# Seven block products for eight in the down projection of segments 1 to 3, and state updates on column halves

## The chip, the cores and the metric

The kernel runs on one core of one Trainium2 chip. The metric is the device time of one execution in microseconds: 3076.15 us, the median of three runs (3075.18 to 3080.12). A core has a matrix engine (PE; its weight loads are listed apart as PEld), a vector engine (DVE), a scalar engine (ACT), a general engine (POOL) and SP, which here issues all DMAs. Each engine takes its own queue in order; between engines there are semaphores.

## The reference

One layer of a streaming encoder on 2048 positions of width 1024, in float32, with 16 meta positions ahead. The part that is changed is the gated MLP at the end, and one matrix product inside the recurrence:

```python
z = rmsnorm(h, norm2_g[l])
u, v = jnp.split(z @ w_up[l], 2, axis=-1)        # D_FF = 2816 columns each: 22 blocks of 128
u = causal_dwconv(u, conv_w[l], conv_b[l])       # width 3, depthwise
h = h + (jax.nn.silu(u) * v) @ w_down[l]         # the down projection, 2816 x 1024
...
S = jnp.exp(a_last[:, :, 0, :])[..., None] * S + jnp.einsum('bhsk,bhsv->bhkv', k_ * jnp.exp(a_last - a_), v_)
```

After the MLP comes a last rmsnorm, and the meta positions are dropped.

## The kernel before

**Tiling.** The 2048 positions go through the whole layer in four segments of 512 (`s` = 0 to 3), each in four row chunks of 128. Every operand of a matrix product is split into a high and a low part (ACT casts the high part, L95 or L108; DVE subtracts for the low one, L96 or L109), and each block takes three matmuls (`PASS`: high x high, high x low, low x high). Weights come by DMA as `raw` tiles (3 buffers) and are split into `w` tiles (3 buffers).

**The MLP** goes through its 22 blocks `j` in groups (`GROUPS`: 8, 8 and 6). In segment 0 a block takes 24 matmuls of 512 columns for `u` and as many for the gate. At the same time `weight_sums` writes sums of weight blocks to DRAM (`s_d`, `a_d`); segments 1 to 3 use them: there `q_open` and `q_rest` build each block by seven products of half size (`seventh`, L779), the Strassen-Winograd scheme, 7 x 12 matmuls of 256 columns. Then DVE and ACT do the convolution, the sigmoid and the gate, and `gated` splits the result into an `act` tile (L109).

**The down projection** of a group follows its blocks in all segments: for each half `dh` of the output columns `rows_product` (L142) multiplies all `act` tiles of the group with the weights, 4 row chunks x 3 matmuls of 512 columns for each block, into four PSUM banks `rp`, which `add_d` then adds to the residual rows `h` (L898). For the very last half, `rows_one_by_one` (L130) goes chunk by chunk, so that `finish` (last rmsnorm and output) can start early.

**The turn of a segment.** Beside the down projection of the last group, the norm of the next segment's input runs: `norm1` hands out five steps (`between`), one at each weight load. A step loads a chunk of x into an `x_row` tile (`xt`, 2 buffers, L69), ACT sums its squares (L171), DVE takes twelve very small steps to the inverse root (`inv_rms`, tiles `nrm`) and scales the chunk (L214); the next step transposes it on PE (`norm1_transposes`, L217, PSUM tag `mm`) and splits it into the `z` tiles (32 per segment on ACT, L111, and 32 on DVE, L112). Then `values` (`rp<-w,z`, L274) starts the next segment and needs all of these.

**Order.** The code is written in the order of the computation; a list scheduler in the tile framework then sets the order of each engine's queue. PSUM has eight banks: tag `mm` has 5 and tag `hg` has 3. What a tile waits for is set by its pool: it gets a buffer when the last user of the buffer is done.

Of the kernel before, what the change touches and what calls it, by code (L numbers as in the profile page):

```python
# [26 lines left out]
GROUPS = ((0, 8), (8, 8), (16, 6))  # L27
# [22 lines left out]
def trunk_layer(ctx: ExitStack, tc: tile.TileContext, x, meta, wts, cst, gf, wpool, out):  # L50
# [79 lines left out]
    def rows_one_by_one(src, chunks, nk, consume):  # L130

        ws = [weights() for _ in range(nk // 2)]
        for ci, (o, n) in enumerate(chunks):
            bank = ps.tile([P, 512], F32, name="rp", tag="hg", bufs=HG)
            for k in range(nk):
                for i, (xi, wi) in enumerate(PASS):
                    T.matmul(bank[:n, :], lhsT=src[k][:, xi, o:o + n],
                             rhs=ws[k // 2][:, wi, (k % 2) * 512:(k % 2 + 1) * 512],
                             start=(k == 0 and i == 0), stop=(k == nk - 1 and i == 2))
            consume(ci, bank)  # L140

    def rows_product(src, chunks, nk, consume, between=(), lo=None, hg=HG):  # L142
# [362 lines left out]
    a_d = [dram.tile([2, P, 2, 512], F32, name=f"a_d{j}") for j in range(NF)]  # L505
    for s in range(nseg):
# [476 lines left out]
```

## Time and profile before

| | |
|---|---|
| median of 3 runs | 3076.15 us |
| the profiled execution, its own time | 3076.68 us |
| its span, first to last instruction | 3074.9 us |
| PE busy | 3023.7 us (98%), 21452 matmuls |
| DVE busy | 1977.5 us (64%) |
| ACT busy | 1296.2 us (42%) |
| DMA | 439.99 MB, 143 GB/s on the mean |

PE's matmuls are pipelined: one of 512 columns is listed with some 390 ns, but in a row they start about 231 ns apart. So the distance from start to start counts, not the length of one. The same holds on DVE, where the next instruction often starts before the listed end of the one before. An average over the run mixes stages; the windows in the rows below are single stages.

### The profile page before, as it was taken

How to read it: one execution, taken by the hardware profiler on the slowest of the kernel's cores; microseconds unless marked ns; L12 is line 12 of the kernel's file. 1: busy time of each engine (PE TensorE's matmuls, PEld its weight loads, DVE VectorE, ACT ScalarE, POOL GpSimd, SP SyncE). 2: the span in 40 equal slices, each digit the busy share in tenths (PEclk: the TensorE clock that was granted, in tenths of full speed). 3: DMA queues.
4: the chain of work that ended last, by engine and by line, in shares of the span. 5: the costliest groups of instructions: out<-in, count | busy, mean ns of one | idle time of the engine just before them, and what ended most of it. 6: DMA issues, size and time to landing. Idle time of an engine off the chain costs nothing.

```text
span 3074.9 us, 51974 instructions
## 1 busy us (share of the span) xinstructions
PE 3023.7 (98%) x21452; PEld 2627.1 (85%) x21452; DVE 1977.5 (64%) x3366; ACT 1296.2 (42%) x2130; POOL 69.3 (2%) x180
## 2 busy tenths in 40 slices
PE   7999999999999999999999999999999999999998
PEld 6999978898887788989987778899898778888987
DVE  5875357565768735857577753685576883485756
ACT  4443234232543424635454332554354432364534
POOL 1000000000000000000000000000000000000000
PEclk9999999999999999999999999999999999999999
DMA  3112238474532225646452222655454212364643
GB/s 142 63 63 76 90 122 292 170 265 175 194 132 70 76 96 165 224 156 218 136 181 74 69 84 96 225 200 171 164 166 151 70 64 95 123 214 167 225 149 110
DMA packets 146497, 439.99 MB, mean 143 GB/s; under 512 B 14018, under 2 KB 14146, under 8 KB 146260
## 3 DMA queue, kind: packets, MB, share of 16 engines
q1 hardware_dynamic: 146260, 436.67, 41.7%
q8 instruction: 168, 2.75, 0.4%
q14 instruction: 69, 0.57, 0.1%
HBM read 382.09 MB, written 54.53 MB: 142 GB/s over the span
## 4 chain that ended last, share of the span: by engine, by line
PE 93%; DVE 3%; DMA 1%; ACT 1%; issue 0%; SPq 0%; DVEq 0%; ACTq 0%
PE pt L124 36%; PE rp L153 22%; PE X L782 12%; PE Y L782 9%; PE pt L749 8%; DMA raw<-in_wts_dram 1%; PE sp L319 1%; PE up L394 1%; PE sp L331 1%; DVE w L96 1%; PE op L408 1%; PE op L413 1%; PE ktp L385 1%; DVE z L109 0%; PE pp L575 0%
## 5 line engine op out<-in xcount | busy, mean ns | idle before, releaser
L96 DVE TENSOR_TENSOR w<-raw,w 128x1024 fp32r<-128x1024 f32 (+1 forms) x607 | 706.6, 1165 | 727.8 <-ACT w L95 724.1
L124 PE MATMUL pt<-z,w 128*128 128x512 f32 (+3 forms) x4800 | 954.7, 354 | 0.0
L124 PEld LDWEIGHTS pt<-z,w 128*128 128x128 f32 x4800 | 773.4, 189 | 136.7 <-issue 12.8
L95 ACT CAST w<-raw 128x1024 fp32r<-128x1024 f32 (+1 forms) x611 | 610.8, 1000 | 650.9 <-PE rp L153 277.2
L153 PE MATMUL rp<-w,act 128*128 128x512 f32 x2040 | 477.2, 394 | 0.0
L153 PEld LDWEIGHTS rp<-w,act 128*128 128x128 f32 x2040 | 381.9, 188 | 87.1
L782 PE MATMUL X<-z,w 128*128 128x256 f32 x2484 | 339.3, 286 | 10.2 <-ACT z L108 5.5
L782 PEld LDWEIGHTS X<-z,w 128*128 128x128 f32 x2484 | 316.7, 194 | 14.3 <-ACT z L108 6.8
L749 PE MATMUL pt<-z,w 128*128 128x256 f32 (+2 forms) x1608 | 254.5, 320 | 0.0
L749 PEld LDWEIGHTS pt<-z,w 128*128 128x128 f32 x1608 | 229.9, 190 | 23.2
L782 PE MATMUL Y<-z,w 128*128 128x256 f32 x1692 | 233.7, 286 | 0.0
L782 PEld LDWEIGHTS Y<-z,w 128*128 128x128 f32 x1692 | 218.5, 195 | 0.3
L153 PE MATMUL rp<-w,mix 128*128 128x512 f32 (+1 forms) x816 | 190.4, 394 | 0.0
L153 PEld LDWEIGHTS rp<-w,mix 128*128 128x128 f32 (+1 forms) x816 | 147.9, 182 | 40.2 <-issue 4.7
L650 ACT ACTIVATE sg<-pt 128x512 f32<-128x512 f32 (+1 forms) x80 | 41.2, 515 | 243.1 <-PE pt L124 243.1
L734 DVE SCALAR_TENSOR_TENSOR cv<-ub,cs,cv 128x512 f32<-128x512 f32 x176 | 131.1, 745 | 0.7
L737 ACT ACTIVATE sg<-cv 128x512 f32<-128x512 f32 x88 | 55.7, 633 | 103.2 <-DVE cv L734 103.1
L153 PE MATMUL rp<-w,z 128*128 128x512 f32 (+1 forms) x408 | 97.9, 398 | 0.0
L124 PE MATMUL pt<-ob,w 128*128 128x512 f32 (+2 forms) x480 | 95.1, 350 | 0.0
L124 PE MATMUL pt<-oa,w 128*128 128x512 f32 (+2 forms) x480 | 94.8, 348 | 0.0
L153 PEld LDWEIGHTS rp<-w,z 128*128 128x128 f32 (+1 forms) x408 | 74.5, 183 | 19.6 <-issue 0.4
L782 PE MATMUL X<-z,wa 128*128 128x256 f32 x684 | 90.9, 281 | 0.0
(197 smaller groups left out, 2902.0 us busy)
## 6 DMA issues: line engine op xcount, KB each, us to landing
raw<-in_wts_dram SPq DMA_DIRECT2D x413, 512.0 KB, 3.5
raw<-s_d SPq DMA_DIRECT2D x132, 512.0 KB, 3.3
wa<-a_d SPq DMA_DIRECT2D x114, 512.0 KB, 5.2
s_d<-ws SPq DMA_DIRECT2D x44, 512.0 KB, 4.5
a_d<-w SPq DMA_DIRECT2D x44, 512.0 KB, 3.7
raw<-in_wts_dram SPq DMA_DIRECT2D x66, 256.0 KB, 3.1
h<-in_x_dram SPq DMA_DIRECT2D x20, 512.0 KB, 6.5
xt<-in_x_dram SPq DMA_DIRECT2D x12, 512.0 KB, 4.3
```

Source lines behind the costliest of these rows:

```text
L95: A.copy(out=w[:, 0, :n], in_=raw[:, :n])
L96: (lo or V).tensor_tensor(out=w[:, 1, :n], in0=raw[:, :n], in1=w[:, 0, :n].bitcast(F32), op=ALU.subtract)
L124: T.matmul(pt[:, :n], lhsT=w[:, wi, (kof + k) * P:(kof + k + 1) * P], rhs=src[k][:, xi, c0 + o:c0 + o + n], start=(k == 0 and i == 0), sto ...
L153: T.matmul(banks[ci][:n, :], lhsT=src[k][:, xi, o:o + n], rhs=w[:, wi, (k % 2) * 512:(k % 2 + 1) * 512], start=(k == 0 and i == 0), stop=( ...
L319: T.matmul(spv[o:o + B, e, c, :], lhsT=k[:, x], rhs=q[:, x], start=True, stop=True)
L331: T.matmul(spv[o:o + h_, e, c, :], lhsT=k[:, x:x + h_], rhs=q[:, x + h_:x + 2 * h_], start=True, stop=True)
L385: T.transpose(out=ktp[:C, c * P:(c + 1) * P], in_=kv[:, c * C:(c + 1) * C], identity=ident)
L650: A.activation(out=sg[:, o:o + n], in_=pt[:, :n], func=AF.Sigmoid)
L734: V.scalar_tensor_tensor(out=cv, in0=ub[:, t_:t_ + SEG], scalar=col(C_CW + t_ * NF, j), in1=cv, op0=ALU.mult, op1=ALU.add)
L737: A.activation(out=sg, in_=cv, func=AF.Sigmoid)
L749: T.matmul(pt[:, po:po + n], lhsT=w[:, wi, k * P:(k + 1) * P], rhs=z2[k][:, xi, c0:c0 + n], start=(k == 0 and i == 0), stop=(k == KB - 1 a ...
L782: T.matmul(dst, lhsT=w[:, wi, kp * P:(kp + 1) * P], rhs=z2[kp][:, xi, xslot], start=(start and kp == 0 and i == 0), stop=(kp == KP - 1 and ...
```

## The change

In segments 1 to 3 the down projection of a group takes seven products instead of eight, again by the Strassen-Winograd scheme. The 2 x 2 blocks are: rows in two halves (chunks 0, 1 and chunks 2, 3), and blocks `j` in pairs (even, odd) against the two halves of the output columns. For each pair of blocks `pair_operands` makes four sums of the gated results and splits what the products need (`act`, four tiles for a pair). The sums of down weights that the scheme needs are made in segment 0 by `down_sums` and written to DRAM (`t_d`). `down_sevenths` runs the seven products, each 3 `nj` matmuls of 512 columns, with its own weight load (`load`: two blocks of 512 columns in one tile), and adds its banks `dp` to `h` (16 adds of 128x512 for a group, 8 before). The groups become 6, 6, 4 and 6. `norm1_transposes` takes its banks from tag `hg`. Tag `am` gets 12 buffers (8 before), tag `zo` 4 (8 before), and `oa` moves to `am`. `pair_operands` keeps its sums in `x_row` tiles. The state update (`upv`) is issued as two matmuls of 64 weight columns for one of 128. `rows_one_by_one` goes.

```diff
@@ trunk_layer
-GROUPS = ((0, 8), (8, 8), (16, 6))
+GROUPS = ((0, 6), (6, 6), (12, 4), (16, 6))
...
-            tp = ps.tile([P, 512], F32, name="tp", tag="mm", bufs=MM)
+            tp = ps.tile([P, 512], F32, name="tp", tag="hg", bufs=HG)
...
-                T.matmul(upv[:, e, c, :], lhsT=kts[e][:C, c * P:(c + 1) * P], rhs=vt[c][:C, v0:v0 + VD],
-                         start=True, stop=True)
+                for d in range(0, P, VD):
+                    T.matmul(upv[d:d + VD, e, c, :], lhsT=kts[e][:C, c * P + d:c * P + d + VD],
+                             rhs=vt[c][:C, v0:v0 + VD], start=True, stop=True)
...
+    t_d = {j0: dram.tile([4, nj // 2, P, 512], F32, name=f"t_d{j0}") for (j0, nj) in GROUPS}
...
-            gated(cv, sy, a)
+            V.tensor_tensor(out=cv, in0=cv, in1=sy, op=ALU.mult)
+            return cv
...
+        def unit():
+            return blk.tile([P, 2, WMAX], F32R, name="act", tag="am", bufs=12)[:, :, :2 * HT].rearrange(
+                "p a (u t) -> p a u t", t=HT)
+
+        def pair_operands(c0, c1, u0):
+            a11, a21, a12, a22 = c0[:, :HT], c0[:, HT:], c1[:, :HT], c1[:, HT:]
+            t = x_row().rearrange("p (u t) -> p u t", t=HT)
+            u1, u2, u3 = unit(), unit(), unit()
+            V.tensor_tensor(out=t[:, 0], in0=a21, in1=a22, op=ALU.add)
+            V.tensor_tensor(out=t[:, 1], in0=a21, in1=a11, op=ALU.subtract)
+            V.tensor_tensor(out=t[:, 2], in0=t[:, 0], in1=a11, op=ALU.subtract)
+            V.tensor_tensor(out=t[:, 3], in0=a12, in1=t[:, 2], op=ALU.subtract)
+            split((u3[:, 0], u3[:, 1]), c1.rearrange("p (u t) -> p u t", t=HT))
+            split((u1[:, 0], u1[:, 1]), t[:, 0:2])
+            split((u2[:, 0], u2[:, 1]), t[:, 2:4])
+            return {"a11": u0[:, :, 0], "a12": u3[:, :, 0], "a22": u3[:, :, 1], "s1": u1[:, :, 0],
+                    "s3": u1[:, :, 1], "s2": u2[:, :, 0], "s4": u2[:, :, 1]}
+
+        def down_sums(j0, nj, dh):
+            def on_raw(i, raw):
+                if i % 2 != dh:
+                    return
+                other = wpl.tile([P, 1024], F32, name="raw", bufs=RAW)
+                nc.sync.dma_start(out=other, in_=wts[M_AT + 3 * j0 + 2 * nj + (1 - dh) * nj // 2 + i])
+                r0, r1 = (other, raw) if dh else (raw, other)
+                t = [blk.tile([P, 2 * WMAX], F32, name="ws", tag="zo", bufs=4)[:, :1024] for _ in range(2)]
+                V.tensor_tensor(out=t[0][:, :512], in0=r1[:, :512], in1=r0[:, :512], op=ALU.subtract)
+                V.tensor_tensor(out=t[0][:, 512:], in0=r1[:, :512], in1=r1[:, 512:], op=ALU.subtract)
+                V.tensor_tensor(out=t[1][:, :512], in0=r1[:, 512:], in1=t[0][:, :512], op=ALU.subtract)
+                V.tensor_tensor(out=t[1][:, 512:], in0=r0[:, 512:], in1=t[1][:, :512], op=ALU.subtract)
+                for o in range(4):
+                    nc.sync.dma_start(out=t_d[j0][o, i], in_=t[o // 2][:, o % 2 * 512:(o % 2 + 1) * 512])
+            return on_raw
+
+        def down_sevenths(ops, j0, nj, between, square, done):
+            nk, pc = nj // 2, M_AT + 3 * j0 + 2 * nj
...
+            def load(src):
+                ws = []
+                for i in range(0, nk, 2):
+                    n = min(2, nk - i)
+                    w = split_weights(src(i, i + n).rearrange("i p f -> p i f"), n * 512, view=True)[0]
+                    ws += [w[:, :, x * 512:(x + 1) * 512] for x in range(n)]
+                return ws
...
+            def product(banks, left, src, start, adds, order=0):
+                ws = load(src)
+                if between:
+                    between.pop(0)()
...
+                for kp, i in seq:
+                    for n, (xi, wi) in enumerate(PASS):
+                        T.matmul(banks[i], lhsT=ops[kp][left][:, xi, i * P:(i + 1) * P], rhs=ws[kp][:, wi, :],
+                                 start=(start and kp == 0 and n == 0), stop=(kp == nk - 1 and n == 2),
+                                 skip_group_check=True)
+                for i in range(2):
+                    for th, dh, final in adds:
+                        v = hx[2 * th + i][:, hcol[dh]]
+                        V.tensor_tensor(out=v, in0=v, in1=banks[i], op=ALU.add)
...
+            X = bank("mm")
+            product(X, "a11", nat(0, 0), True, ((0, 0, 0),))
+            product(bank("hg"), "a12", nat(0, 1), True, ((0, 0, 1),))
+            product(X, "s2", cat(2), False, ((0, 1, 0),))
+            Y = bank("mm")
+            product(Y, "s1", cat(0), True, ((1, 1, 0),))
+            product(X, "s3", cat(1), False, ((1, 1, 1), (1, 0, 0)))
+            product(Y, "s4", nat(1, 1), False, ((0, 1, 2),))
+            product(bank("hg"), "a22", cat(3), True, ((1, 0, 2),), order=1)
...
-                    q_rest(j, at_u(j) + 1, *opened.pop(j), act[j - j0])
+                    cv = q_rest(j, at_u(j) + 1, *opened.pop(j))
+                    if j % 2 == 0:
+                        even, u0 = cv, unit()
+                        split((u0[:, 0, 0], u0[:, 1, 0]), cv[:, :HT])
+                    else:
+                        ops.append(pair_operands(even, cv, u0))
...
-            for dh in range(2):
...
-                if end and dh == 1:
-                    rows_one_by_one(act, rows, nj, add_d)
-                else:
-                    rows_product(act, rows, nj, add_d, chunks)
+            if first_s:
+                for dh in range(2):
...
+                    rows_product(act, [(c * P, P) for c in range(NCH)], nj, add_d, chunks, on_raw=down_sums(j0, nj, dh))
+            else:
+                down_sevenths(ops, j0, nj, chunks, square, lambda ci: finish(ci, 1) if end else None)
```

Three places show how the queues change.

First, PE in the last group of segment 0 (`rp<-w,act` is its down projection, `tp` the transposes of the next input, `rp<-w,z` the start of the next segment). Before:

```order
L153 MATMUL rp<-w,act 128x512 x24
L221 MATMUL tp<-ident,xt 128x128 x8
L153 MATMUL rp<-w,act 128x512 x28
L221 MATMUL tp<-ident,xt 128x128 x8
L153 MATMUL rp<-w,act 128x512 x41
L221 MATMUL tp<-ident,xt 128x128 x8
L153 MATMUL rp<-w,act 128x512 x31
L221 MATMUL tp<-ident,xt 128x128 x8
L153 MATMUL rp<-w,act 128x512 x20
L153 MATMUL rp<-w,z 128x512 x96
```

and now:

```order
L144 MATMUL rp<-w,act 128x512 x67
L212 MATMUL tp<-ident,xt 128x128 x4
L144 MATMUL rp<-w,act 128x512
L212 MATMUL tp<-ident,xt 128x128 x4
L144 MATMUL rp<-w,act 128x512 x4
L212 MATMUL tp<-ident,xt 128x128 x16
L144 MATMUL rp<-w,act 128x512 x67
L212 MATMUL tp<-ident,xt 128x128 x4
L144 MATMUL rp<-w,act 128x512
L212 MATMUL tp<-ident,xt 128x128 x4
L144 MATMUL rp<-w,act 128x512 x4
L144 MATMUL rp<-w,z 128x512 x96
```

The transposes were spread over both halves of the down projection; now the first three chunks stand together between the two halves, and the last at the end.

Second, DVE at the end of the last group's blocks in segment 1 (`cv` is the gated result, `sy` the last read of a block's products, `act` splits, `nrm` the small steps of the norm, `xt` with `nrm` the scaling of a chunk of x, `w` the low part of a weight tile). Before, at the last block but one and the last:

```order
L109 TENSOR_TENSOR act_14270<-cv_14874,act_14270 128x512
L165 TENSOR_TENSOR nrm_15053<-nrm_15053 128x1
L166 SCALAR_TENSOR_TENSOR nrm_15053<-nrm_15053 128x1
...
L214 TENSOR_SCALAR xt_15046<-xt_15046,nrm_15053 128x1024
L96 TENSOR_TENSOR w_15039<-raw_15037,w_15039 128x1024
L814 TENSOR_TENSOR ub_14996<-Y_14907,sx_14908 128x512
L96 TENSOR_TENSOR w_15093<-raw_15091,w_15093 128x1024
L734 SCALAR_TENSOR_TENSOR cv_15000<-ub_14996,cs_91,cv_15000 128x512
L820 TENSOR_TENSOR sy_14981<-X_14906,sy_14981 128x512
```

and now, from the last block on:

```order
L814 TENSOR_TENSOR cv_15420<-cv_15420,sy_15401 128x512
L826 TENSOR_TENSOR xt_15446<-cv_15293,cv_15420 128x256
...
L109 TENSOR_TENSOR act_15448<-xt_15446,act_15448 128x512
L168 TENSOR_TENSOR nrm_15488<-ss_15483 128x1
...
L205 TENSOR_SCALAR xt_15481<-xt_15481,nrm_15488 128x1024
L168 TENSOR_TENSOR nrm_15567<-ss_15562 128x1
...
L155 SCALAR_TENSOR_TENSOR nrm_15567<-nrm_15567 128x1
L96 TENSOR_TENSOR w_15531<-raw_15529,w_15531 128x512
L883 TENSOR_TENSOR h1_11507<-h1_11507,dp_15465 128x512
L883 TENSOR_TENSOR h1_11509<-h1_11509,dp_15466 128x512
```

The norm of the first two chunks stood ahead of the last block's end; now it stands behind its splits, and ahead of the low part `w_15531` of the second product's last weight tile.

Third, DVE at the end of a group that is not the last, segment 1, from the last block's `sy` on. Before:

```order
L820 TENSOR_TENSOR sy<-X,sy 128x512
L734 SCALAR_TENSOR_TENSOR cv<-ub,cs,cv 128x512
L96 TENSOR_TENSOR w<-raw,w 128x1024
L738 TENSOR_TENSOR cv<-cv,sg 128x512
L742 TENSOR_TENSOR cv<-cv,sy 128x512
L109 TENSOR_TENSOR act<-cv,act 128x512
L96 TENSOR_TENSOR w<-raw,w 128x1024 x3
```

and now, in the group of four:

```order
L813 TENSOR_TENSOR sy<-X,sy 128x512
L727 SCALAR_TENSOR_TENSOR cv<-ub,cs,cv 128x512
L883 TENSOR_TENSOR h_11507<-h_11507,dp 128x512
L883 TENSOR_TENSOR h_11509<-h_11509,dp 128x512
L96 TENSOR_TENSOR w<-raw,w 128x1024
L731 TENSOR_TENSOR cv<-cv,sg 128x512
L96 TENSOR_TENSOR w<-raw,w 128x1024
L814 TENSOR_TENSOR cv<-cv,sy 128x512
L826 TENSOR_TENSOR xt<-cv 128x256
L828 TENSOR_TENSOR xt<-xt,cv 128x256
L109 TENSOR_TENSOR act<-cv,act 128x512
```

Between the last block's product and its split there are now two adds, two sums and one more weight tile.

## Rows read from the trace of the kernel before

**Rows 1.** The page, part 1, whole run: busy us (share) xinstructions.

```profile
span 3074.9 us, 51974 instructions
...
PE 3023.7 (98%) x21452; PEld 2627.1 (85%) x21452; DVE 1977.5 (64%) x3366; ACT 1296.2 (42%) x2130; POOL 69.3 (2%) x180
```

**Rows 2.** The page, part 4: the chain that ended last, by engine.

```profile
PE 93%; DVE 3%; DMA 1%; ACT 1%; issue 0%; SPq 0%; DVEq 0%; ACTq 0%
```

**Rows 3.** Groups by line, forms apart: count | busy us, mean ns | idle before.

```profile
L153 PE MATMUL rp<-w,act 128*128 128x512 f32 x2040 | 477.2, 394 | 0.0
```

**Rows 4.** Windows: from:to, length, PE PEld DVE ACT POOL busy, PEclk, DMA, GB/s.

```profile
1300.90:1321.04 20.14, 20.14 (x172) 20.14 (x170) 15.61 (x21) 12.05 (x21) 0.62 (x5) 1.00 0.75 249
1321.04:1365.45 44.41, 44.41 (x194) 36.09 (x193) 19.35 (x22) 10.00 (x11) 0.00 (x0) 1.00 0.33 111
1549.90:1587.20 37.30, 37.23 (x179) 30.44 (x178) 31.88 (x91) 25.04 (x63) 1.07 (x1) 1.00 0.47 156
810.10:847.00 36.90, 36.90 (x177) 30.20 (x176) 28.86 (x91) 23.77 (x61) 0.00 (x0) 1.00 0.40 129
...
3030.96:3064.50 33.54, 33.54 (x147) 26.98 (x145) 22.35 (x55) 10.75 (x21) 0.00 (x0) 1.00 0.26 91
```

**Rows 5.** Timeline, PE, last group of segment 1: start, length, instruction, count.

```profile
1555.46 1.03 PE L221 MATMUL tp<-ident,xt 128*128 128x128 f32 x8
...
1587.05 3.19 PE L153 MATMUL rp<-w,z 128*128 128x512 f32 x13
```

**Rows 6.** Timeline, DVE, segment 1: start us, length us, instruction, count.

```profile
1379.15 0.69 DVE L738 TENSOR_TENSOR cv<-cv,sg 128x512 f32<-128x512 f32 x1
1379.88 0.69 DVE L742 TENSOR_TENSOR cv<-cv,sy 128x512 f32<-128x512 f32 x1
...
1545.16 0.16 DVE L164 SCALAR_TENSOR_TENSOR nrm<-nrm 128x1 f32<-128x1 f32 x1
1545.36 0.16 DVE L165 TENSOR_TENSOR nrm<-nrm 128x1 f32<-128x1 f32 x1
...
1548.05 1.22 DVE L96 TENSOR_TENSOR w<-raw,w 128x1024 fp32r<-128x1024 f32 x1
1549.19 0.68 DVE L814 TENSOR_TENSOR ub<-Y,sx 128x512 f32<-128x512 f32 x1
...
1552.21 0.74 DVE L734 SCALAR_TENSOR_TENSOR cv<-ub,cs,cv 128x512 f32<-128x512 f32 x1
1552.87 1.22 DVE L96 TENSOR_TENSOR w<-raw,w 128x1024 fp32r<-128x1024 f32 x1
...
1558.19 0.60 DVE L112 SCALAR_TENSOR_TENSOR z<-tp,cs,z 128x128 fp32r<-128x128 f32 x2
...
1586.29 1.88 DVE L898 TENSOR_TENSOR h<-h,rp 128x512 f32<-128x512 f32 x3
```

**Rows 7.** Timeline, ACT, before the last group of segment 1.

```profile
1540.90 0.59 ACT L171 ACTIVATE jk<-xt 128x512 f32<-128x512 f32 x1
1541.44 0.19 ACT L171 ACTIVATION_READ_ACCUMULATOR jk<-xt 128x1 f32 x1
...
1545.10 0.62 ACT L108 CAST act<-cv 128x512 fp32r<-128x512 f32 x1 [0.37 <-DVE cv L742]
```

**Rows 8.** DMA issues, KB each, median us to landing.

```profile
xt<-in_x_dram SPq DMA_DIRECT2D x12, 512.0 KB, 4.3
```

**Rows 9.** Timeline, SP, early in the MLP of segment 1.

```profile
1240.01 0.38 SPq L209 DMA_DIRECT2D xt<-in_x_dram  x1
```

**Rows 10.** Windows, to_z2 in segment 1 (columns as in rows 4).

```profile
1246.35:1253.06 6.71, 3.41 (x16) 2.21 (x14) 4.89 (x8) 2.46 (x3) 0.00 (x0) 0.83 0.99 357
1253.06:1258.00 4.94, 4.94 (x25) 4.94 (x25) 1.23 (x1) 1.69 (x3) 0.00 (x0) 0.55 0.85 296
```

**Rows 11.** Timeline, PE, a state update in segment 1.

```profile
913.19 2.00 PE L394 MATMUL up<-vt,kt 128*128 128x64 f32 x16
...
917.06 0.39 PE L408 MATMUL op<-at,vt 128*64 128x128 f32 x4
```

More of the change, by code (lines that the diff above doesn't have):

```diff
@@ L128, in proj, with rows_product @@
         return res
[L130 to L142, printed above, removed]
+    def rows_product(src, chunks, nk, consume, between=(), lo=None, hg=HG, on_raw=None):
         banks = [ps.tile([P, 512], F32, name="rp", tag="hg", bufs=HG) if i < hg else
@@ L568, in trunk_layer @@
             chunks_out(p, q, k, tot, main, vt[-NCH:], False, o_raw)
-        ob = [blk.tile([P, 2, WMAX], F32R, name="ob", tag="zo") for _ in range(4)]
+        ob = [blk.tile([P, 2, WMAX], F32R, name="ob", tag="zo", bufs=4) for _ in range(4)]
         def group_product(g, dt):
@@ L620, in trunk_layer @@
         rsqrt(rs, ms, n1, n2)
-        rss = blk.tile([P, 2, WMAX], F32R, name="rss", tag="am")
+        rss = blk.tile([P, 2, WMAX], F32R, name="rss", tag="am", bufs=12)
         split((rss[:8, 0, :W1], rss[:8, 1, :W1]), rs)
-        oa = [blk.tile([P, 2, WMAX], F32R, name="oa", tag="zo") for _ in range(PAIRS)]
+        oa = [blk.tile([P, 2, WMAX], F32R, name="oa", tag="am", bufs=12) for _ in range(PAIRS)]
         for p in range(PAIRS):
@@ L640, in trunk_layer @@
             split((oa[p][:, 0, :W1], oa[p][:, 1, :W1]), t1[:, :W1])
-        mix = [blk.tile([P, 2, WMAX], F32R, name="mix", tag="am") for _ in range(KB)]
+        mix = [blk.tile([P, 2, WMAX], F32R, name="mix", tag="am", bufs=12) for _ in range(KB)]
         for d in range(KB):
@@ L790, in q_open @@
             else:
-                a11, a12 = (blk.tile([P, 2, WMAX], F32R, name="wa", tag="zo")[:, :, :512] for _ in range(2))
+                a11, a12 = (blk.tile([P, 2, WMAX], F32R, name="wa", tag="zo", bufs=4)[:, :, :512] for _ in range(2))
                 for i, a in enumerate((a11, a12)):
@@ L823, in trunk_layer @@
         for (j0, nj) in GROUPS:
-            act = [blk.tile([P, 2, WMAX], F32R, name="act", tag="am") for _ in range(nj)]
+            act = [blk.tile([P, 2, WMAX], F32R, name="act", tag="am", bufs=12) for _ in range(nj if first_s else 0)]
             at_u = lambda j: M_AT + 3 * j0 + 2 * (j - j0)
             if not first_s:
-                opened = {}
+                opened, ops = {}, []
                 for j in range(j0, j0 + nj):
@@ L893, in finish, with square, add_d @@
                         nc.sync.dma_start(out=out[s * SEG + c * P:s * SEG + (c + 1) * P], in_=hx[c])
-            for dh in range(2):
-                def add_d(ci, bank):
-                    v = hx[ci][:, dh * 512:(dh + 1) * 512]
-                    V.tensor_tensor(out=v, in0=v, in1=bank, op=ALU.add)
-                    if last:
-                        square_sums(ss[:, dh, ci:ci + 1], v, P)
-                    if end and dh == 1:
-                        finish(ci, 1)
-                rows = [(c * P, P) for c in range(NCH)]
-                if end and dh == 1:
-                    rows_one_by_one(act, rows, nj, add_d)
-                else:
-                    rows_product(act, rows, nj, add_d, chunks)
+            def square(ci, dh, v):
+                if last:
+                    square_sums(ss[:, dh, ci:ci + 1], v, P)
+            if first_s:
+                for dh in range(2):
+                    def add_d(ci, bank):
+                        v = hx[ci][:, dh * 512:(dh + 1) * 512]
+                        V.tensor_tensor(out=v, in0=v, in1=bank, op=ALU.add)
+                        square(ci, dh, v)
+                    rows_product(act, [(c * P, P) for c in range(NCH)], nj, add_d, chunks, on_raw=down_sums(j0, nj, dh))
+            else:
+                down_sevenths(ops, j0, nj, chunks, square, lambda ci: finish(ci, 1) if end else None)
             if last and not end:
```

34 lines of the change are left out of this document (24 added, 10 removed).

## The prediction

> **What bounds the kernel now.** I read the page's busy shares first, then the chain of waits, then single stages in windows. PE is busy for 98% of the span, and the chain that ended last is PE for 93% [rows 1, 2]; DVE has 64% on the mean. So the time is PE's, and the question for a change that takes matmuls off PE and gives work to DVE is whether DVE keeps up stage by stage. In the windows the reader is to look for PE's busy time against the length (no gap) and for DVE's beside it [rows 4]. The down projection of the first group of segment 1 takes 44.41 us for 192 matmuls, 0.231 us each, with DVE at 19.35. A stretch of two blocks has DVE at 15.61 of 20.14. But in the last group, where the norm of the next input runs beside it, DVE is at 31.88 of 37.30 (28.86 of 36.90 in segment 0) and PE has still no gap. That stage has nearly no room on DVE.
>
> **The change, part by part.** Time counts from T, when PE is done with a group's last block. DVE's steps are from start to start [rows 6]: a weight split of 1024 takes 1.14 us (1548.05 to 1549.19), an operation of 512 takes 0.60 (three adds in 1.88, the last 0.69 long) or 0.73 where it needs the one before, a convolution step 0.66, a small `nrm` step 0.20 in a chain, a `z` split 0.26 to 0.30. ACT casts 512 in 0.62 and squares half a chunk in 0.59 + 0.19 [rows 7]. For operations of 256 I take 0.4.
>
> *Matmuls.* Down projection: 24 matmuls for a block become 21; the lines that issue them are in [rows 3]. Saved are 3 x 22 x 3 segments = 198 x 0.231 = 45.8 us: 15.3 in a segment, 11.1 of it in the first three groups (16 blocks), 4.2 in the last.
>
> *First three groups.* For six blocks DVE now has 7 x (1.14 + 0.60) of weights and 16 x 0.60 of adds, 21.8 us, beside 126 x 0.231 = 29.1 of PE: room on the mean. But DVE works in order, and the second product's last third needs the last block's split. In the first group DVE's queue from T is `sy` 0.60, weights 0.60 and 1.14, convolution 0.66, weights 0.60, convolution 0.66, two adds 1.2, gate 0.73, weights 1.14, product 0.73: 8.1; the cast 0.62 makes 8.7, the low part 9.7. PE is there after 30 matmuls, at 7.0: 2.5 lost. In the second group the weights stand later, and I get 0.8. In the group of four PE wants the same at 18 x 0.231 = 4.2; DVE has `sy` and a convolution, waits for the first product's banks (adds until 3.6), then a weight tile, gate, a weight tile, product: 7.4, cast 8.0: 3.8 lost. Its fifth product finds its weights behind adds that wait for the fourth (17.4 + 1.14 against 16.6): 1.9 more; with small ones 6.0. Together 9.3 of the 11.1: 1.8 gained in each of three segments, **-5.4**. Bounds: -33.3 with no wait at all, +10 if each wait is half as long again. I take the walk, since the queue's order is fixed and each duration has a row.
>
> *Blocks.* A pair of blocks costs DVE now 4 x 0.4 more for sums and 0.34 + 2 x 0.6 - 0.6 for splits, about 2.5 on 15.61 of 20.14 [rows 4]: hidden by PE's seven products; if that cover went, 33 pairs x 2.5 would show.
>
> *Last group, segments 1 and 2.* Two things come late. First, chunk loads of x: before, the first was issued at 1240.01, 310 us ahead [rows 9], since `x_row` was free. Now `pair_operands` holds both buffers through the blocks, and SP has weight loads ahead of the x load: the first x goes out at about T + 4, lands 4.3 later [rows 8], has its squares at 10.0, twelve chained steps 2.4 and the scaling 0.67: 13.1. PE has its first 18 matmuls done at 4.2 and the transposes stand next: 8.9 us idle. Queued behind the waiting `nrm` on DVE are the weights of the second product. The second chunk's buffer is that of the last pair, free at 8.2: landed at 12.8, squares 14.4, ten steps 16.4, then `w_15531` 17.0, and the second product ends at 18.0. Second, from there DVE is the bound: until the next segment's first weights 6 x 1.14 + 5 x 0.60 of weights, 15 adds 9.0, 32 `z` splits 8.9, 26 small steps between other work at half price 2.6, three scalings 2.0: 32.4, and a us of waits for ACT. So the next segment starts at T + 50.4, before T + 37.3 (1549.9 to 1587.2) [rows 4, 5]: 13.1 lost, twice, **+26**. Bounds for one: -5.0, if PE alone counted (126 x 0.231 + 32 transposes at 0.1 = 32.3); +9.7 if DVE had all its work (47 us from T) and no wait; +17 if the waits are longer.
>
> *Last group, segment 0.* Matmuls stay; DVE gets 12 sums of 512, 7.2 us, on 28.86 of 36.90, hidden if nothing else moves. But `tp` now shares three banks with the product's own. PE transposes the first chunk only after 67 matmuls (15.5) and an add, until 16.5. Only then is its `x_row` buffer free for the third chunk: issued 16.9, landed 21.2, squares 22.8, small steps between `z` splits 26.0, scaling 26.7, transposes 27.5. All this stands ahead of the second half, which could start at 72 x 0.231 + 2.4 = 19.0: 8.5 lost, and some at the end: **+9**. Bounds 0 and +12. The other sums of segment 0 (32 of 0.60, 11 more loads of 512 KB, 44 stores of 256 KB) lie beside PE's 24 matmuls a block; I take +1, bounds 0 and +6.
>
> *Last group, segment 3.* 4.2 saved, 2.2 lost as in the second group, and the end: two chunks finish together, adds, squares, two mixed chains of steps and four scalings, some 10 us behind the last matmul instead of 7. **0**, bounds -4 and +4. It was 33.54 [rows 4].
>
> *State updates.* 16 records in 1.93 (913.19 until the next instruction at 915.12) [rows 11] become 32 on half the columns. The nearest row is `op`, which already goes on column halves: 4 in 0.22, 0.055 each, so 1.76: 0.17 x 16 updates, **-2.7**; bounds -3.4 and +3.4 (0.067 each, the pace of the 64-column score products). The Trainium skill ("TensorEngine Tiling (Array Packing)", Theoretical Speedup) gives up to two times for a dimension of 64: by it, as an estimate, an update takes 0.97 and 15 us are gained in all, and the forecast would be 3094; the measured 0.055 for an instruction does not bear it out.
>
> *Clock.* Where PE was busy for 3.41 of 6.71 us, the granted clock was 0.55 in the next 4.94 us, that is mostly the lower level, 1.2 GHz, and 25 matmuls of 256 took 4.94 [rows 10], some 2 us more than at the full clock. Idle stretches of 8 to 9 us now come in three places: **+2** in all, since DVE mostly hides it; bounds 0 and +10.
>
> Sum: -5.4 + 26 + 9 + 1 + 0 - 2.7 + 2 = +29.9 on the span of 3074.9: 3104.8; with the 1.8 us that the profiled execution has beside its span, 3106.6. It is 0.5 above the median of the runs: **3106 us**, 1.0% slower.
>
> **Rivals.**
> *A, faster: PE stays the bound everywhere.* For it: no gap in any row of PE, and DVE's 64%. Then 45.8 + 2.7 go: 3028. If only the last groups behave by DVE's load without waits (+9.7 twice) and the first three groups lose nothing (-33.3), with segment 0 at 0 and -2.7: 3060. Against it: 47 us of DVE work in a stage that took 37.3. The Trainium skill ("Perfetto Trace Analysis", Identifying the Most-Contended Engine) says to optimize the engine with the highest occupancy first; by it the change hits the right engine and gives 3028. The trace agrees for the run, but not for the last groups. Chance 0.21.
> *B, no change:* the last groups lose as forecast and the first three groups keep their 33.3, since the waits there are shorter than walked: 3106 - 28 = 3078. Chance 0.13.
> *C, much slower: the lower clock decides.* If after each idle stretch the products run at the lower level, as in rows 10, while DVE waits for their banks, each of the three last groups loses 4 more, and the weight queue of segment 0, with SP waiting for sums before it issues loads, another 6: 3123. It decides as soon as DVE waits for PE there. Chance 0.14.
> That the change doesn't do what it says is excluded by the queue: 126 matmuls `dp` stand for 144.
>
> **Numbers.** The forecast itself has 0.52, its own range is 3090 to 3122. About 0.2%, 6 us, is what a measurement of this kernel can tell from no change. Slower by more: 0.52 + 0.14 = 0.66; within: 0.13; faster: 0.21. The range that leaves out 2 in 10 reaches from 3064 (into A, past B) to 3130 (past C).
>
> **What the profile will show.** If I am right: `dp` matmuls at 0.231 apart with gaps of 2 to 6 us at the second product; in the last groups of segments 1 and 2 a stop of some 9 us behind the first 18 matmuls, DVE over 90% busy, and about 50 us from T to the next segment; in segment 0 a stop of 8 us between the halves. I am wrong if PE is without gaps there, if the last groups take under 42 us, or if the blocks of segments 1 to 3 take over 10.1 us each.

## The result and the profile after

The changed kernel takes 3098.01 us (median of 4 runs, 3095.28 to 3099.68), the kernel before 3078.07 beside it (3075.18 to 3080.12): ratio 1.0065, 95% interval 1.0047 to 1.0082. It is slower by 20 us; 3106 was forecast, in a range of 3064 to 3130.

The page of the changed kernel: busy time and share of each engine, then the chain that ended last.

```profile
PE 2989.5 (97%) x21526; PEld 2578.7 (83%) x21526; DVE 2202.5 (71%) x3817; ACT 1373.9 (44%) x2277; POOL 77.3 (2%) x180
...
PE 81%; DVE 9%; DMA 5%; ACT 4%; issue 1%; SPq 0%; DVEq 0%; ACTq 0%
```

PE is busy for 2989.5 us where 45.8 us of matmuls are gone, and the chain, 93% PE before [rows 2], now goes through DVE, DMA and ACT for 18%. Where this comes from shows when the span is cut at the last groups of the four segments. The first fence is the kernel before, the stretches between the last groups; the second the kernel after, the same stretches and then the last groups of segments 0 to 3 (columns as in rows 4: length, PE, PEld, DVE, ACT, POOL busy, granted clock, DMA share, GB/s).

```profile
0.00:810.10 810.10, 782.14 (x6044) 701.64 (x6045) 492.41 (x895) 295.51 (x487) 20.43 (x46) 0.99 0.43 151
847.10:1549.90 702.80, 698.76 (x4913) 602.51 (x4912) 455.45 (x714) 305.48 (x479) 14.47 (x51) 1.00 0.42 141
1587.10:2290.80 703.70, 699.19 (x4914) 602.56 (x4913) 455.53 (x714) 305.47 (x480) 15.04 (x51) 1.00 0.42 141
2327.90:3031.10 703.20, 698.95 (x4914) 602.68 (x4913) 453.59 (x701) 304.62 (x476) 17.25 (x30) 1.00 0.42 140
```

```profile
0.00:805.40 805.40, 776.82 (x6124) 697.28 (x6125) 519.20 (x939) 294.69 (x487) 20.40 (x46) 0.99 0.48 170
854.40:1551.80 697.40, 688.73 (x4928) 590.28 (x4929) 508.59 (x819) 325.15 (x518) 19.12 (x52) 1.00 0.45 150
1604.80:2301.80 697.00, 687.63 (x4930) 587.55 (x4930) 508.69 (x814) 325.28 (x514) 19.27 (x52) 1.00 0.46 152
2355.10:3052.10 697.00, 689.17 (x4930) 590.13 (x4929) 508.33 (x814) 324.95 (x514) 18.16 (x30) 1.00 0.46 152
...
805.40:854.40 49.00, 40.05 (x177) 31.45 (x176) 33.22 (x93) 22.56 (x59) 0.00 (x0) 0.90 0.46 163
1551.80:1604.80 53.00, 37.67 (x160) 29.47 (x159) 43.89 (x124) 31.87 (x79) 0.21 (x1) 0.87 0.48 153
2301.80:2355.10 53.30, 38.71 (x160) 29.76 (x159) 43.84 (x124) 31.69 (x79) 0.16 (x1) 0.84 0.47 153
3052.10:3096.30 44.20, 30.76 (x128) 22.74 (x126) 36.78 (x96) 17.72 (x33) 0.00 (x0) 0.93 0.46 153
```

All stretches between the last groups got shorter: by 4.7, 5.4, 6.7 and 6.2, 23.0 together. The last groups got longer: segment 0's from 36.9 to 49.0, segment 1's from 37.3 to 53.0 [rows 4], segment 2's as much, segment 3's by half a us; 44.5 together. 44.5 - 23.0 is the 21.5 by which the span grew (3074.9 to 3096.4).

In a last group, what stops PE is seen in its timeline (start, us, instruction, in brackets the idle time before it and who ended it), here segment 1:

```profile
1551.82 4.31 PE L877 MATMUL dp<-w,act 128*128 128x512 f32 x18
1566.06 1.97 PE L212 MATMUL tp<-ident,xt 128*128 128x128 f32 x8 [9.93 <-DVE xt L205]
1567.68 3.56 PE L877 MATMUL dp<-w,act 128*128 128x512 f32 x8
```

18 matmuls, then 9.93 us of nothing until the scaled first chunk of x is there. The chain behind it, one step on each engine: SP issues the loads of x, ACT squares, DVE makes the small steps and scales. SP's timeline of the changed kernel:

```profile
1555.86 5.02 SPq L200 DMA_DIRECT2D xt<-in_x_dram  x2
```

ACT's, the first square:

```profile
1561.57 0.60 ACT L162 ACTIVATE jk<-xt 128x512 f32<-128x512 f32 x1 [1.78 <-DMA xt<-in_x_dram]
```

DVE's, from the splits of the last pair of blocks (the first line) on:

```profile
1559.06 1.46 DVE L109 TENSOR_TENSOR act<-xt,act 128x512 fp32r<-128x512 f32 x2
1562.94 0.16 DVE L168 TENSOR_TENSOR nrm<-ss 128x1 f32<-128x1 f32 x1 [2.42 <-ACT jk L162]
...
1565.25 0.75 DVE L205 TENSOR_SCALAR xt<-xt,nrm 128x1024 f32<-128x1024 f32 x1
...
1567.73 0.69 DVE L96 TENSOR_TENSOR w<-raw,w 128x512 fp32r<-128x512 f32 x1
```

The load goes out 4.0 us behind the start of the stage (T + 4 in the prediction), and the low part of the second product's last weight tile stands behind the `nrm` steps and is done at 1568.42, T + 16.6 (17.0 in the walk).

In segment 0 PE's timeline shows the transposes of three chunks between the two halves, the second and third waiting:

```profile
823.34 0.66 PE L212 MATMUL tp<-ident,xt 128*128 128x128 f32 x4
826.74 1.10 PE L212 MATMUL tp<-ident,xt 128*128 128x128 f32 x4 [2.75 <-DVE z L112]
833.80 1.97 PE L212 MATMUL tp<-ident,xt 128*128 128x128 f32 x8 [5.97 <-DVE xt L205]
835.42 1.91 PE L144 MATMUL rp<-w,act 128*128 128x512 f32 x4
```

### The profile page after: what moved, and what is told of

Same layout as the page of the kernel before. It is cut to its first block, busy times and chain, and to the rows that moved or that the text cites. A ratio compares the mean times of both kernels' runs of the same rounds, so it can differ in the third digit from the quotient of the medians.

```text
span 3096.4 us, 53221 instructions
## 1 busy us (share of the span) xinstructions
PE 2989.5 (97%) x21526; PEld 2578.7 (83%) x21526; DVE 2202.5 (71%) x3817; ACT 1373.9 (44%) x2277; POOL 77.3 (2%) x180
## 3 DMA queue, kind: packets, MB, share of 16 engines
q1 hardware_dynamic: 176596, 479.93, 45.8%
## 4 chain that ended last, share of the span: by engine, by line
PE 81%; DVE 9%; DMA 5%; ACT 4%; issue 1%; SPq 0%; DVEq 0%; ACTq 0%
PE pt L124 34%; PE rp L144 12%; PE X L775 10%; PE pt L742 8%; PE Y L775 7%; PE dp L877 7%; DVE w L96 2%; ACT w L95 1%; DMA raw<-in_wts_dram 1%; DMA raw<-t_d 1%; PE sp L310 1%; DMA xt<-in_x_dram 1%; DMA raw<-s_d 1%; DVE xt L268 1%; PE op L405 1%
## 5 line engine op out<-in xcount | busy, mean ns | idle before, releaser
L96 DVE TENSOR_TENSOR w<-raw,w 128x1024 fp32r<-128x1024 f32 (+1 forms) x688 | 768.2, 1121 | 566.3 <-ACT w L95 565.4
L95 ACT CAST w<-raw 128x1024 fp32r<-128x1024 f32 (+1 forms) x692 | 667.5, 967 | 599.4 <-PE rp L144 181.1
L877 PE MATMUL dp<-w,act 128*128 128x512 f32 x1386 | 347.7, 404 | 19.1 <-DVE w L96 10.6
L877 PEld LDWEIGHTS dp<-w,act 128*128 128x128 f32 x1386 | 257.9, 192 | 94.0 <-DVE w L96 19.0
L775 PEld LDWEIGHTS X<-z,w 128*128 128x128 f32 x2484 | 314.7, 192 | 13.9 <-DVE z L109 4.7
L883 DVE TENSOR_TENSOR h<-h,dp 128x512 f32<-128x512 f32 x192 | 124.9, 681 | 24.9 <-PE dp L877 24.7
L144 PE MATMUL rp<-w,act 128*128 128x512 f32 x528 | 125.0, 396 | 0.0
L144 PEld LDWEIGHTS rp<-w,act 128*128 128x128 f32 x528 | 99.6, 189 | 23.0 <-DVE z L112 0.3
```

The costliest lines, as they stand in the source:

```text
L95: A.copy(out=w[:, 0, :n], in_=raw[:, :n])
L96: (lo or V).tensor_tensor(out=w[:, 1, :n], in0=raw[:, :n], in1=w[:, 0, :n].bitcast(F32), op=ALU.subtract)
L144: T.matmul(banks[ci][:n, :], lhsT=src[k][:, xi, o:o + n], rhs=w[:, wi, (k % 2) * 512:(k % 2 + 1) * 512], start=(k == 0 and i == 0), stop=( ...
L775: T.matmul(dst, lhsT=w[:, wi, kp * P:(kp + 1) * P], rhs=z2[kp][:, xi, xslot], start=(start and kp == 0 and i == 0), stop=(kp == KP - 1 and ...
L877: T.matmul(banks[i], lhsT=ops[kp][left][:, xi, i * P:(i + 1) * P], rhs=ws[kp][:, wi, :], start=(start and kp == 0 and n == 0), stop=(kp == ...
L883: V.tensor_tensor(out=v, in0=v, in1=banks[i], op=ALU.add)
```

## Experiments

Each was timed beside the kernel before (medians of 3077.1 to 3077.7 there).

**e1_inplace.** Is the stop in the last groups the late load of x?

```diff
-            t = x_row().rearrange("p (u t) -> p u t", t=HT)
+            t = tpl.tile([P, 512], F32, name="xs", tag="t").rearrange("p (u t) -> p u t", t=HT)
...
-            V.tensor_tensor(out=t[:, 1], in0=a21, in1=a11, op=ALU.subtract)
-            V.tensor_tensor(out=t[:, 2], in0=t[:, 0], in1=a11, op=ALU.subtract)
-            V.tensor_tensor(out=t[:, 3], in0=a12, in1=t[:, 2], op=ALU.subtract)
+            V.tensor_tensor(out=a21, in0=a21, in1=a11, op=ALU.subtract)
+            V.tensor_tensor(out=a11, in0=t[:, 0], in1=a11, op=ALU.subtract)
+            V.tensor_tensor(out=t[:, 1], in0=a12, in1=a11, op=ALU.subtract)
...
-            split((u2[:, 0], u2[:, 1]), t[:, 2:4])
+            split((u2[:, 0], u2[:, 1]), c0.rearrange("p (u t) -> p u t", t=HT))
...
```

> The changed kernel, but the pair sums no longer take an x_row buffer: two of the four are written over the even block's gated result, the other two into a small scratch tile; same sums, same products. So x of the next segment can be loaded before the last group ends.
> Theory L (late x): the stop of 10.1 us in front of the first transposes of the last groups of segments 1 and 2 comes from x being loaded only when the pair sums give back their buffer. Then the stop goes, DVE (43.9 us busy of 53.0 there) becomes the bound, the two last groups come down to 42 to 47 us each, and the whole falls by 12 to 22 us against the changed kernel, to about 3080.
> Rival D (DVE's work alone): the stage is as long as DVE's queue, the stop only moves, the last groups stay above 50 and the whole falls by less than 6 us.

3087.34 us, ratio 1.0035 (1.0022 to 1.0047): 10.7 below the changed kernel, a little less than theory L had at the least. PE's timeline in segment 1 and the windows of the last groups of segments 1 and 2:

```profile
1556.63 4.33 PE L877 MATMUL dp<-w,act 128*128 128x512 f32 x18
1560.80 1.03 PE L212 MATMUL tp<-ident,xt 128*128 128x128 f32 x8
1561.59 3.31 PE L877 MATMUL dp<-w,act 128*128 128x512 f32 x11
```

```profile
1556.60:1601.00 44.40, 35.31 (x160) 26.40 (x159) 41.53 (x112) 31.32 (x75) 0.28 (x1) 1.00 0.50 166
2298.80:2347.20 48.40, 39.52 (x161) 29.95 (x160) 41.54 (x112) 31.70 (x75) 0.21 (x1) 0.89 0.50 162
```

The first transposes no longer wait, so the stop was the late x. What is left points at DVE, busy for 41.53 of 44.40; PE's waits there are shared between ACT's weight casts (3.7), DVE's adds (2.6) and DVE's weight splits (2.0), and e7_thin_adds below tells which of them is behind the others. The two segments run the same instructions, with 41.5 us of DVE in each; the second took 4.0 longer at a granted clock of 0.89. So the gain was 8.6 in one stage and 4.9 in the other.

**e2_tp_seg0.** Are the stops of segment 0 the shared banks?

```diff
-            tp = ps.tile([P, 512], F32, name="tp", tag="hg", bufs=HG)
+            tp = ps.tile([P, 512], F32, name="tp", tag=tag, bufs=HG if tag == "hg" else MM)
...
-                later.append(norm1_chunk(x[s * SEG + c * P:s * SEG + (c + 1) * P], P, c * P, dst))
+                later.append(norm1_chunk(x[s * SEG + c * P:s * SEG + (c + 1) * P], P, c * P, dst, "mm" if s == 1 else "hg"))
```

> The changed kernel, but in the last group of segment 0 alone the transposes of the next x go back to the banks of tag mm, as before the change.
> Theory B (banks): the 9.2 us of stops between the two halves there come from the transposes sharing three banks with the product. Then the stage falls from 49.0 us to 37 to 39 and the whole by 10 to 12 us.
> Rival S (sums): the 12 sums of 512 on DVE and their loads make the stage long. Then it stays above 45 and the whole falls by less than 4 us.

3085.66 us, ratio 1.0029 (1.0018 to 1.0041): 12.4 less. The window of that last group:

```profile
803.10:840.50 37.40, 37.16 (x178) 30.21 (x177) 31.68 (x93) 22.10 (x56) 0.00 (x0) 1.00 0.62 213
```

37.4 for 49.0, with all sums still on DVE (31.68; 28.86 before the change [rows 4]). The sums cost half a us there; the banks cost the rest.

**e3_last8.** Does all of the loss sit in the three last groups?

```diff
+                later.append(norm1_chunk(x[s * SEG + c * P:s * SEG + (c + 1) * P], P, c * P, dst, "mm"))
...
+                plain = j0 + nj == NF and s < nseg - 1
...
+                    if plain:
+                        a = act[j - j0]
+                        split((a[:, 0, :SEG], a[:, 1, :SEG]), cv)
...
-            if first_s:
+            if first_s or (j0 + nj == NF and s < nseg - 1):
```

> The changed kernel with the last group of segments 0, 1 and 2 as before the change: in segments 1 and 2 that group by eight products (no pair sums in it), and the transposes of the next x in the banks of tag mm. Segment 3 and the first three groups of segments 1 to 3 keep the seven products.
> Theory (the loss sits in the three last groups): they come back to about 37 us each, that is -12, -16 and -16 us; the whole is about 3054, 22 below the kernel before, and what is left is the gain of the first three groups (14) and of the state updates (9).
> Rival (smaller groups, or buffers held elsewhere, make the loss): the last groups stay above 42 and the whole falls by less than 25 us.

3052.11 us, ratio 0.9919 (0.9906 to 0.9933): 45.9 below the changed kernel and 25 below the one before. The last groups of segments 1 and 2:

```profile
1536.10:1573.20 37.10, 37.07 (x179) 30.29 (x178) 31.71 (x91) 24.97 (x63) 1.07 (x1) 1.00 0.46 156
2271.20:2308.40 37.20, 37.12 (x178) 30.33 (x178) 31.76 (x92) 25.00 (x63) 1.05 (x1) 1.00 0.46 157
```

PE has practically no gap (37.07 busy of 37.10), with 18 matmuls more in each than the seven products have, and the clock is 1.00. In segments 1 and 2 this run puts back the eight products and the banks together; what the banks alone cost there was not tried.

**e4_up_only.** What is the state update's edit worth by itself?

```diff
-                T.matmul(upv[:, e, c, :], lhsT=kts[e][:C, c * P:(c + 1) * P], rhs=vt[c][:C, v0:v0 + VD],
-                         start=True, stop=True)
+                for d in range(0, P, VD):
+                    T.matmul(upv[d:d + VD, e, c, :], lhsT=kts[e][:C, c * P + d:c * P + d + VD],
+                             rhs=vt[c][:C, v0:v0 + VD], start=True, stop=True)
```

> The kernel before, with one edit: each state update's matmul is two on the column halves of the array.
> Forecast's term: -2.7 us. By the pitch of the heads in the changed kernel (34.1 for 35.2 us in segment 0, 32.0 for 32.35 behind it) it is -8 us. If two instructions on column halves ran side by side and nothing else waited, 32 records in 0.95 for 16 in 1.7 us, it would be -12 us or more.

3068.57 us, ratio 0.9973 (0.9964 to 0.9983): -8.6. The timeline of PE at the update of rows 11:

```profile
904.65 1.18 PE L395 MATMUL up<-vt,kt 128*64 128x64 f32 x32
905.66 0.39 PE L409 MATMUL op<-at,vt 128*64 128x128 f32 x4
905.88 0.39 PE L414 MATMUL op<-q,st 128*64 128x128 f32 x4
906.10 0.39 PE L409 MATMUL op<-at,vt 128*64 128x128 f32 x4
906.71 0.43 PE L414 MATMUL op<-q,sc 128*64 128x128 f32 x2 [0.22 <-DVE sc L402]
```

32 halves are through in 1.01 us (904.65 to 905.66), 16 whole ones took 1.93 [rows 11]. In the trace the halves start in pairs, 7 ns apart, and the next pair 58 ns later (904.757 and 904.764, 904.816 and 904.822); whole ones start 112 ns apart. One after another, halves would also take 58 ns each: so the score products `sp` of the same form start in the kernel before, which all go to one half (909.213, 909.271, 909.330, and so on):

```profile
909.11 1.15 PE L331 MATMUL sp<-q,k 128*64 128x64 f32 x16
```

So a half takes about half the time of a whole one, and two halves run side by side. But then the output products come to a state that DVE has not made yet (`sc`).

**e5_op_order**, and **e8_op_start** with the same instructions in the same order. Does the wait for `sc` eat part of it?

```diff
-                         rhs=a_t[:, e, c, :], start=True, stop=first)
-            if not first:
+                         rhs=a_t[:, e, c, :], start=(c == 0), stop=first, skip_group_check=True)
+        if not first:
+            for c in range(n):
                 for e in range(2):
...
```

These are the lines of e8_op_start, on top of e4's edit; e5_op_order has `start=True` in place of `start=(c == 0)`.

> The kernel before with the state updates on column halves (as in e4_up_only, 3068.6 us), and one more edit: of the output products behind each update the 8 that need no state (op<-at,vt) are issued first and the 8 that read the states (op<-q,st and op<-q,sc) after them.
> Theory W (the halves ran side by side, and part of what they saved turned into a wait for DVE's chain of states): in e4_up_only the update took 1.01 us for 1.93, but the output products behind it 3.07 for 2.47, with the first sc product 1.05 us behind the update's end. With 16 us-cheap products in front (16 records by 0.055 are 0.9 us) the wait goes, 0.3 to 0.6 us at each of 16 updates: 5 to 10 us below e4_up_only, about 3061.
> Rival: the output products are slow for another reason (the halves of the array, not DVE). Then it stays within 2 us of e4_up_only.

> As e5_op_order, with one difference: of the output products that need no state only the first of each half of the array begins a new sum in the bank (the order of e5_op_order lets a later one begin anew and so drops what the earlier ones had written: its output left those terms out). Same instructions and order.
> Theory W: the same time as e5_op_order, 3061 us, 7 below e4_up_only, since the order alone makes the time.
> Rival: the gain of e5_op_order hung on the terms that it left out; then it is back at 3068.

3061.28 us (0.9949, 0.9937 to 0.9962) and 3061.76 us (0.9950, 0.9936 to 0.9963): 7 below e4_up_only, and the terms left out played no part. PE's timeline in e8_op_start at the same update:

```profile
907.17 1.18 PE L395 MATMUL up<-vt,kt 128*64 128x64 f32 x32
908.18 1.04 PE L409 MATMUL op<-at,vt 128*64 128x128 f32 x16
909.05 0.39 PE L415 MATMUL op<-q,st 128*64 128x128 f32 x4
909.27 0.96 PE L415 MATMUL op<-q,sc 128*64 128x128 f32 x8
```

The wait is gone at this update; on the whole PE's waits for `sc` between 840 and 1170 us are 0.7 in e4_up_only and none in e8_op_start.

**e7_thin_adds.** What holds the seven products once x is early? On the base of e1_inplace:

```diff
-                        V.tensor_tensor(out=v, in0=v, in1=banks[i], op=ALU.add)
+                        V.tensor_tensor(out=v[:, :1], in0=v[:, :1], in1=banks[i][:, :1], op=ALU.add)
```

> The kernel with pair sums in place (e1_inplace, 3087.3 us), but each add of a product to the rows of h in segments 1 to 3 takes one column of 512 (so most of the down projection's result is left out): same instructions and waits, 16 of them in a group some 0.5 us shorter on DVE.
> Theory V (DVE's queue is the bound in the last groups, and the waits of the first three groups are DVE's too): the last groups of segments 1 and 2 fall from 44.4 and 48.4 by 5 to 8 us each, the first three groups by 2 to 5 us in a segment; 15 to 30 us in all.
> Rival T (transfers and casts of the weights, not DVE's adds, hold the products up): less than 2 us in a last group and less than 1 in the others; under 7 us in all.

3061.73 us, ratio 0.9952 (0.9938 to 0.9965): 25.6 below e1_inplace. The last groups of segments 1 and 2, and the down projection of segment 1's first group (31.6 in the changed kernel):

```profile
1551.20:1591.70 40.50, 36.78 (x161) 28.12 (x160) 34.75 (x112) 31.11 (x77) 0.24 (x1) 0.92 0.59 183
2285.20:2325.40 40.20, 36.47 (x160) 28.32 (x159) 34.86 (x112) 31.12 (x77) 0.24 (x1) 0.92 0.60 184
1309.00:1338.60 29.60, 29.60 (x129) 23.59 (x128) 20.65 (x41) 14.52 (x19) 0.71 (x2) 1.00 0.63 192
```

7 us less on DVE make the last groups 3.9 and 8.2 us shorter (in the second, e1_inplace had lost 4.0 to the clock), the first three groups are shorter by 3.9, 2.5 and 2.4 in segments 1 to 3, and the first group's products run without a gap. In the first of the two last groups that is less than the 5 us that theory V had at the least, and in the second about half of the 8.2 is the clock's. But rival T allowed under 2, and PE's waits for ACT's weight casts there fell from 3.7 to 0.8 with the casts unchanged: DVE's queue held both up, which is theory V with its size too high for the last groups. 40.5 is still 3 above the eight products of the kernel before; what holds the rest (a stop of 3.0 is put down to the scaling of x, and the clock is 0.92) was not tried further.

**e6_best** and **e9_best2.** Do the gains add up? e6_best has the sums in place and the output products of e5_op_order (and leaves out the terms that this does); e9_best2 has the sums in `x_row` and the output products of e8_op_start. Both have the last groups of e3_last8.

> All that helped together: the changed kernel with eight products and the banks of tag mm in the last groups of segments 0 to 2 (e3_last8, 3052.1 us), pair sums in place (e1_inplace), and the output products in the order of e5_op_order.
> If the edits add up: e3_last8 less 5 to 10 us from the output products, and 0 to -2 from the sums in place, since where these won, in the last groups, there are none now: about 3044.
> Rival: the scratch tile of the sums in place takes a buffer that the blocks need (in e1_inplace the first three groups were 1 to 2 us longer in a segment), and the output products gain nothing: 3052 to 3057.

> e3_last8 (3052.1 us) with the output products in the order of e8_op_start, and with the pair sums in x_row as in the changed kernel (e6_best had them in place).
> If the edits add up: 3052 less 5 to 8 us, about 3045.5, some 3 us below e6_best (3048.8), because the sums in place cost 1 to 2 us in a segment's first three groups.
> Rival (the sums in place cost nothing, and the output products gain only 3 us beside the other edits): the same as e6_best within 1 us.

3048.82 us (0.9909, 0.9893 to 0.9924) and 3048.18 us (0.9908, 0.9894 to 0.9921). Both are 28 to 29 us below the kernel before and 49 to 50 below the changed one. But by the medians the order of the output products is worth only 3 to 4 us here, where it was 7 on the kernel before (the intervals leave room for either), and that the sums in place cost something is not borne out: in both points e9_best2 went its rival's way.

## Why the prediction was right

The mechanisms of the two large terms came as forecast, but that the whole came within 8 us (3106 for 3098) is partly luck, since misses cancelled. On the span, the last groups were to cost 35 and cost 44.5; the first three groups were to gain 5.4 and gained 13.9; state updates and the sums of segment 0 were to gain 1.7 together, and what is left of the gain in the other stretches is 9.1; the clock's 2 is inside the last groups. These misses are +9.5, -8.5, -7.4 and -2, 8.4 less than forecast in all. Two of the signs that were named did not come either: in the first three groups no gap of the `dp` matmuls was over 0.53 us where 2 to 6 were announced at the second product, and in the last groups of segments 1 and 2 DVE was busy for 83% (43.89 of 53.00), not over 90%.

*Slower, and where:* the sum put +35 into the last groups of segments 0 to 2; they were +44 (12.1, 15.7, 16.2), and e3_last8 gives back 45.9.

*Last groups, segments 1 and 2 (+13.1 each).* Late x, then DVE: e1_inplace shows the first, e7_thin_adds the second. The stop was 9.93 us (8.9 forecast), and the stage 53.0 where 50.4 was forecast. Part of the difference is the clock behind the stop, which the sum had at +2 for the whole kernel: the window of the first 5.1 us of PE's work after it, and the one behind segment 0's stop.

```profile
1565.90:1571.00 5.10, 4.94 (x16) 4.26 (x17) 4.79 (x17) 1.69 (x4) 0.00 (x0) 0.51 0.26 86
835.40:837.20 1.80, 1.80 (x7) 1.47 (x6) 1.62 (x9) 1.25 (x4) 0.00 (x0) 0.55 0.00 0
```

The granted clock is 0.51, the lower level of 1.2 GHz, and there the eight transposes took 1.62 us (1566.06 to 1567.68) for 0.80 to 0.85 at the later chunks. That is rival C's mechanism; it came with the forecast, not in its place.

*Last group, segment 0 (+9).* The stops were 2.75 and 5.97, 8.7 together (8.5 forecast); the stage lost 12.1. e2_tp_seg0 shows the banks as the cause of all but half a us; that half is the sums, which the forecast had as hidden. Behind the stops comes a stretch at the lower clock (0.55 in the second line above), which goes with them.

*First three groups (-5.4): mis-sized, -13.9.* From the first product to the last group the three groups of segments 1 to 3 take 244.7, 244.7 and 243.5 us where 14 blocks and two products took 228.9, 229.1 and 228.8 and two blocks 20.0 (eight blocks take 80.05 us, 1365.45 to 1445.50 in the kernel before): 4.2, 4.4 and 5.3 gained. The walk had 9.3 us of waits in a segment; the 336 matmuls took 82.2, and 0.231 each would be 77.6. The groups by line in segment 1 (count, busy us, mean ns, idle before and who ended it), in the changed kernel:

```profile
L877 PE MATMUL dp<-w,act 128*128 128x512 f32 x336 | 82.2, 397 | 2.1 <-DVE w L96 1.3 <-DVE h L883 0.4 <-ACT w L95 0.3
```

and in e7_thin_adds:

```profile
L877 PE MATMUL dp<-w,act 128*128 128x512 f32 x336 | 79.5, 395 | 0.8 <-ACT act L108 0.8
```

The waits are DVE's, as walked: 1.7 of 2.1 us are put down to it, and thin adds take most of them away. The step that failed is PE's queue in the walk, most of all in the group of four, where 6.0 was forecast and 1.4 to 1.8 came. There PE was to stand after 18 matmuls, at T + 4.2, until DVE's product and ACT's cast of the last block were done at T + 8.0. In segment 1 (T = 1469.38) PE's timeline and ACT's cast are:

```profile
1469.38 5.25 PE L877 MATMUL dp<-w,act 128*128 128x512 f32 x22
...
1477.79 4.46 PE L877 MATMUL dp<-w,act 128*128 128x512 f32 x18
```

```profile
1477.11 0.62 ACT L108 CAST act<-cv 128x512 fp32r<-128x512 f32 x1 [3.13 <-DVE cv L814]
```

The cast is done at T + 8.35, so DVE's side of the walk holds. But PE was busy until then: between the two lines stand 8 more `dp` matmuls and 12 of the next group's first blocks. 30 `dp` matmuls and these 12 are 8.3 us of work (0.231 and 0.117 each). Without the last block the first two products have only 18, so 12 of the 30 belong to later products, whose first pair of blocks was ready: the queue puts them ahead of the last pair, where the walk took the products one after another. The other groups have 7 and 12 block matmuls among their products. In segment 1 PE also stops for 1.3 us in two places among the blocks, put down to ACT's `sx`, which the walk had as hidden.

*State updates (-2.7): mis-sized, -8.6 alone.* I took 0.055 us for a half, the pace of the output products. These go side by side in pairs, as the halves of the update do, but each streams 128 columns, and a half of the update streams 64; it takes 0.031 (1.01 / 32). The Trainium skill ("TensorEngine Tiling (Array Packing)", Theoretical Speedup) was right where the row that I put against it was not comparable: the update took 1.01 where the estimate by it was 0.97. Of the 15 us that this gives, 6 did not arrive; e5_op_order brings back 7 by putting work in front of DVE's chain of states. The -8.6 is between medians. The two profiles differ by some 5 us in their clock alone (see below), but the distance from update to update, which that stretch doesn't enter, says the same: in e4_up_only it is 34.1 for 35.2 us in segment 0 and 32.0 for 32.35 behind it, some 8 us for the 16 updates.

*Segment 3 (0)* was +0.5. *Rival A* fell for the reason given against it: DVE in the last groups. None of the kernels here reached its 3028; e9_best2 is 20 above it. Rival C's terms add up to 3124, not 3123.

What stays open: the kernel before and the changed one show a granted clock of 0.90 and 0.93 in a stretch of segment 0 whose instructions no edit here changes, and other kernels 1.00; so 3 to 5 us of any single profile need not be the edit's. The window of that stretch in the kernel before:

```profile
220.00:270.00 50.00, 49.88 (x354) 46.68 (x353) 34.02 (x59) 19.14 (x37) 0.75 (x1) 0.90 0.23 74
```

in the changed kernel:

```profile
220.00:270.00 50.00, 49.88 (x370) 46.98 (x369) 34.47 (x60) 18.53 (x34) 0.00 (x0) 0.93 0.22 75
```

and in e2_tp_seg0 (e4_up_only is like it, x395 at 1.00):

```profile
220.00:270.00 50.00, 49.88 (x395) 47.15 (x394) 37.01 (x64) 20.33 (x37) 0.00 (x0) 1.00 0.22 75
```

In 50 us at the full clock PE issued 395 matmuls, at 0.90 only 354: 41 fewer, or 5 us. The shorter updates don't decide it: the changed kernel and e2_tp_seg0 both have them, and they differ only in the last group of segment 0, some 530 us later. What does decide it was not found.

## What to carry to other kernels

Matmuls taken off a PE-bound kernel are worth what the tightest stage lets through: look at the other engines' load stage by stage, and leave the old form where they are already full (here the last groups, worth 46 us together with the old banks). When a scratch tile is put in an old tag, ask who else allocates from it and when: two borrowed buffers, `x_row` (13.5 us in e1_inplace) and the banks of tag hg (11.6 in e2_tp_seg0), made over half of the 44 us that the last groups lost. And a saving on PE in front of a dependent chain on DVE came in full on the kernel before only when work that needs no result of the chain stood behind it.

## What the runs showed of the hardware

Two matmuls of 64 output columns on the two column halves run side by side: in e4_up_only a pair of them takes 58 ns, what one of the same form takes in the kernel before when all go to one half, and one of 128 output columns takes 112 ns. So 32 halves take 1.01 us where 16 whole ones took 1.93. The price goes with the columns streamed too: the output products, in pairs as well but with 128 columns streamed for 64, take 0.055 each for 0.031.

And the same stop need not cost the same clock: in e1_inplace segments 1 and 2 run the same instructions in their last groups, at a granted clock of 1.00 in one and 0.89 in the other, which is 4.0 us of 48.4.
